# Attention stage of a hybrid encoder step: sums and transposes in halves of one bank, more places for the sums' copy, later output transposes

## The chip, the cores and the metric

The kernel runs on one core of a Trainium2 chip. The metric is the device time of one execution in microseconds (us); less is better. Engine names: TensorE is PE in the profile (its weight loads are PEld), VectorE is DVE, ScalarE is ACT, GpSimd is POOL, SyncE is SP, which issues the DMAs here.

## What is computed

One layer of an encoder step for 1024 prompt frames and 64 sample frames of width 1024. The combined input projection feeds three head groups: six heads of forgetting attention (softmax, called fox), a gated MLP over 128-frame chunks (sgu), and six heads of stick-breaking attention (sb). Their outputs are normalised per head and go through one output projection; then follow a layer norm, a squared-ReLU MLP of width 4096 and a second layer norm. What the change touches is the attention:

```python
def fox_block(q, c_q, qpos, k, v, c_k):
    s = jnp.einsum('bqhd,bkhd->bhqk', q, k) / math.sqrt(D_HEAD)
    s = s + c_q - c_k
    p = jax.nn.softmax(jnp.where(mask, s, NEG_INF), axis=-1)
    return jnp.einsum('bhqk,bkhd->bqhd', p, v)

def sb_block(q, qpos, k, v):
    z = jnp.einsum('bqhd,bkhd->bhqk', q, k) / math.sqrt(D_HEAD)
    log_rem = jnp.where(mask, jax.nn.log_sigmoid(-z), 0.0)
    after = lax.cumsum(log_rem, axis=3, reverse=True) - log_rem
    a = jnp.where(mask, jnp.exp(jax.nn.log_sigmoid(z) + after), 0.0)
    return jnp.einsum('bhqk,bkhd->bqhd', a, v)
```

The arithmetic is float32: a matrix product is made of passes over high and low parts of its operands (`PASSES`).

## The kernel before

The kernel has three stages. The first interleaves all input projections (a generator `fill`) with the attention of both groups (a generator `attn`); a loop at its end asks now one and now the other for its next step by running costs. The second is the output projection with the first norm (`mix`), whose first two row blocks are still asked for by `fill`. The third is the MLP.

A scheduling layer under the kernel orders each engine's instructions by its own estimate of times and by the buffers that are free, and derives the semaphores. So the order in which the kernel's lines are traced is a proposal: the built program may hold another.

Attention runs by pairs of heads (three fox pairs, then three sb pairs); each pair has units (u, h): query block pair u of four, head h of two, and at the end one unit for the sample frames. A unit has three parts:

- `a_steps`: scores of two blocks of 128 queries into banks with tag `s` (L561), then the weights: for fox T by VectorE and an exponential, for sb sg and sn by two sigmoids, a scan (L545) and a product on GpSimd (L547).
- `b_steps`: the weights are transposed 256 keys at a time into banks `pt` (L609) and copied as high and low parts into `pth` by ScalarE (L577) and VectorE (L98). Four products (L619 to L622) add them to the unit's sum `o` of 128 x 256, which takes one bank. Then ScalarE copies the sum into `osb` (L632), which has one place.
- `c_step`: the copy is transposed by two instructions (L640) into `otp`, in the bank with tag `tr`; VectorE adds its high and low halves into `ot` (L641), and after the second head a DMA stores `ot` in DRAM.

The bank `tr` is also used for the transposes of the keys: `pk` (L486) for the prompt and the cached keys (`pkc`, L678) for the sample. `o` is also used by the sample's sum (L741, L745). Each of the tags `o` and `tr` has one bank (bufs=1).

`attn` traces a unit's `b_steps` and the next unit's `a_steps` by turns. A unit's `c_step` goes on a list, which is worked off while the next unit's steps are traced:

```python
                    k += 1
                    if k == 2 and c_pend:
                        while c_pend:
                            c_pend.pop(0)()
```

`prep` loads rows of `o_dr` and of the gates `uu` for the output projection; for the first two row blocks (MIXED) `uu` lies in the pool `sa` with two places.

Of the kernel before, what the change touches and what calls it, by code (L numbers as in the profile page):

```python
# [12 lines left out]
F32 = mybir.dt.float32  # L13
# [7 lines left out]
P = 128  # L21
# [35 lines left out]
def _build(nc, tc, a, es):  # L57
# [117 lines left out]
    def prep(t, sa):  # L175
        n = trows(t)
        o = two_halves(f"oo{t}", sa, "kp")
        if sa is not None:
            uu = sa.tile([P, 256], F32, name=f"uu{t}", tag="uu", bufs=2)
            sqs = [sa.tile([P, 512], F32, name=f"sq{t}", tag="sq", bufs=1)] * 2  # L180
        else:
            uu = sp.tile([P, 256], F32, name=f"uu{t}", tag="gl", bufs=3)
            sqs = [sp.tile([P, 512], F32, name=f"sq{t}_{i}", tag="raw", bufs=2) for i in range(2)]
        nc.sync.dma_start(uu[0:n], u_dr[t * P:t * P + n, :])
        ss = sp.tile([P, 16], F32, name=f"ss{t}", tag="ss", bufs=2)
        for i in range(2):
            oh = o[i][0:n]
            nc.sync.dma_start(oh, o_dr[t * P:t * P + n, i * 512:(i + 1) * 512])
            c = slice(384, 512) if i == 0 else slice(0, 128)
            nc.gpsimd.tensor_tensor(oh[:, c], oh[:, c], uu[0:n, i * P:(i + 1) * P], op=ALU.mult)  # L190
            sq = sqs[i]
            nc.scalar.activation(sq[0:n], oh, AF.Square)
            sh = ss[0:n, i * 8:(i + 1) * 8]
            nc.vector.tensor_reduce(sh, sq[0:n].rearrange("p (h c) -> p h c", c=DH), axis=AX.X, op=ALU.add)
            nc.vector.scalar_tensor_tensor(sh, sh, 1.0 / DH, env["rge"][0:n, t, i * 8:(i + 1) * 8],
                                           op0=ALU.mult, op1=ALU.add)
            nc.gpsimd.tensor_tensor(sh, sh, negh[0:n].broadcast_to([n, 8]), op=ALU.pow)
            o3 = oh.rearrange("p (h c) -> p h c", c=DH)
            nc.vector.tensor_tensor(o3, o3, sh.unsqueeze(2).broadcast_to([n, 8, DH]), op=ALU.mult)
        os_[t] = o  # L200
# [83 lines left out]
    ps = es.enter_context(tc.tile_pool(name="ps", bufs=2, space=PSUM))  # L284
# [4 lines left out]
    gmx = sp.tile([P, KT], F32, name="gmx")  # L289
    with ExitStack() as p1:  # L290
        sa = p1.enter_context(tc.tile_pool(name="sa", bufs=1, side="right"))
        sel2 = sa.tile([TS, P], F32R, name="sel2")
        nc.vector.tensor_copy(sel2[:, 0:TS], ident[0:TS, 0:TS])
        nc.vector.tensor_copy(sel2[:, TS:P], ident[0:TS, 0:TS])
# [156 lines left out]
        def kv_stage(st, tiles, kpiece, vpiece):  # L451
            j, wkv, nv = st["nm"], st["wkv"], st["nv"]
            kcol = st["hp"] * P
            kvs = []
            for i, t in enumerate(tiles):
                n = trows(t)
                if st["first"]:
                    x_trans(t, xrs[t])
                acc = ps.tile([P, 512], F32, name=f"kv{j}_{t}", tag="acc", bufs=2)
                yield from tok_mm(acc, 0, wkv, t, 0, nv)  # L460
                kv = sa.tile([P, 256], F32, name=f"kvs{j}_{t}", tag="kvs", bufs=2)
                kvs.append(kv)
                nc.scalar.activation(kv[0:n], acc[0:n, 0:256], AF.Copy)
                if nv > 256:
                    nc.vector.tensor_copy(fx[0:n, t, :], acc[0:n, 256:262])
                if t == NB:
                    fold(nc.vector, kv[0:n], acc, 0, 256)
                    if nv > 256:
                        fold(nc.vector, fx[0:n, t, :], acc, 256, 6)
                g = 0 if t < NB else 1  # L470
                r0 = t * P if t < NB else 0
                nc.sync.dma_start(flat(st["ok"][g])[r0:r0 + n, kcol:kcol + P], kv[0:n, 0:P])
                nc.sync.dma_start(flat(st["ov"][g])[r0:r0 + n, kcol:kcol + P], kv[0:n, P:2 * P])
                vs = kv[0:n, P:2 * P].rearrange("p (h c) -> p h c", h=2)
                vh = vpiece[0:n, i, :, 0:DH]
                nc.gpsimd.tensor_copy(vh, vs)
                lo_sub(nc.gpsimd, vpiece[0:n, i, :, DH:P], vs, vh)
                if i + 1 < len(tiles):
                    yield 0.109 * 8

            def finish():
                tot = 0
                pk = ps.tile([P, 2 * P], F32, name=f"pk{j}_{tiles[0]}", tag="tr", bufs=1)
                for kv, t in zip(kvs, tiles):
                    n = trows(t)
                    nc.tensor.transpose(pk[:, tot:tot + n], kv[0:n, 0:P], ident[0:n, 0:n])  # L486
                    tot += n
                k_stack(pk[:, 0:tot], kpiece, tot, f"{j}_{tiles[0]}")

            later.append(finish)  # L490
            yield 0.109 * 8

# [87 lines left out]
        class Unit:  # L580
# [18 lines left out]
            def b_steps(self):  # L599
                st, u, h, rows = self.st, self.u, self.h, self.rows  # L600
                nm = f"{st['nm']}_{u}_{h}"
                o = ps.tile([P, 256], F32, name=f"o{nm}", tag="o", bufs=1)
                pths = {}

                def tr(m):
# [22 lines left out]
                    av(m - 1)  # L628
                    yield 0.88
                av(u)  # L630
                osb = sa.tile([P, 256], F32, name=f"osb{nm}", tag="osb", bufs=1)
                nc.scalar.activation(osb, o, AF.Copy)  # L632

                def c_step():
                    if h == 0:
                        st["ot"] = sa.tile([P, 2, P], F32, name=f"ot{nm}", tag="ot", bufs=1)
                    ot = st["ot"]
                    otp = ps.tile([P, 2, P], F32, name=f"otp{nm}", tag="tr", bufs=1)
                    for half in range(2):
                        nc.tensor.transpose(otp[:, half, :], osb[:, half * P:(half + 1) * P], ident)  # L640
                    nc.vector.tensor_reduce(ot[:, :, h * DH:(h + 1) * DH],  # L641
                                            otp.rearrange("p q (s c) -> p q c s", s=2), axis=AX.X, op=ALU.add)
                    if h == 1:
                        oc = st["ocol"]
                        nc.sync.dma_start(o_dr[u * 256:(u + 1) * 256, oc:oc + P].rearrange("(q p) c -> p q c", p=P), ot)
                        written.add((st["nm"], u))
# [6 lines left out]
        class Sample:  # L653
# [16 lines left out]
            def prep_steps(self):  # L670
                st = self.st
                nm = st["nm"]
                self.kc = [sa.tile([P, 2, 256], F32R, name=f"kc_{nm}_{m}", tag="kp", bufs=10) for m in range(2)]
                self.vc = [sa.tile([P, 2, 2, P], F32R, name=f"vc_{nm}_{m}", tag="vp", bufs=10) for m in range(2)]
                for m in range(2):
                    pk = ps.tile([P, 256], F32, name=f"pkc{nm}_{m}", tag="tr", bufs=1)
                    for t in range(2):
                        nc.tensor.transpose(pk[:, t * P:(t + 1) * P], self.kr[m][:, t, :], ident)  # L678
                    k_stack(pk, self.kc[m], 256, f"c{nm}_{m}")
                    for t in range(2):  # L680
                        vh, vl = self.vc[m][:, t, :, 0:DH], self.vc[m][:, t, :, DH:P]
                        vr = self.vr[m][:, t, :].rearrange("p (h c) -> p h c", h=2)
                        nc.gpsimd.tensor_copy(vh, vr)
                        lo_sub(nc.gpsimd, vl, vr, vh)
                    yield 0.22
# [37 lines left out]
            def b_steps(self):  # L723
                st = self.st
                nm, vn, vc, row = st["nm"], st["vn"], self.vc, self.row
                nk = PAST + TS
                o = ps.tile([P, 256], F32, name=f"os{nm}", tag="o", bufs=1)
                pt = ps.tile([P, 512], F32, name=f"pts{nm}", tag="pt", bufs=2)
                for kb in range(NPB):
                    nc.tensor.transpose(pt[:, kb * P:(kb + 1) * P], row[:, kb * P:(kb + 1) * P], ident)  # L730
# [264 lines left out]
        def attn():  # L995
# [39 lines left out]
            def settle(x):  # L1035
# [7 lines left out]
                if x[1] == 4:  # L1043
                    live["kn"] -= 1

            nxt = a_of(seq[0])
            yield from nxt
            for i, x in enumerate(seq):
                b = x[3].b_steps()
                nxt = a_of(seq[i + 1]) if i + 1 < len(seq) else iter(())  # L1050
                alive = [nxt, b]
                k = 0
                while alive:
                    g = alive[k % len(alive)]
                    try:
                        c = next(g)
                    except StopIteration:
                        alive.remove(g)
                        continue
                    if isinstance(c, tuple) and c not in done:  # L1060
                        for cb_ in b:
                            yield cb_
                        settle(x)
                    yield c
                    k += 1
                    if k == 2 and c_pend:
                        while c_pend:
                            c_pend.pop(0)()
                settle(x)
            while c_pend:  # L1070
                c_pend.pop(0)()

        c_pend = []
        nc.scalar.preload_act_table_set("natural_log_exp_and_others")
# [1059 lines left out]
```

## Time and profile before

| | us |
|---|---|
| median of 3 runs | 1394.44 |
| lowest and highest | 1392.70, 1396.25 |
| the profiled execution | 1397.22 |
| its span, first to last instruction | 1395.4 |
| mean granted TensorE clock in it | 0.984 of full speed |

The profile is of one execution. Engine times in it are busy times within the span; a wait is an engine's idle time, told with the instruction that ended it. The granted clock is the share of TensorE's full speed that the throttle allowed. L-numbers are lines of the kernel before; L98 is a helper that subtracts a high part (`lo_sub`).

### The profile page before, as it was taken

The page shows a single profiled execution, that of the slowest core. Times are in us where ns is not written, and L with a number is a line of the kernel's source. Part 1 is how long each engine was busy: PE and PEld are TensorE (multiplying, and loading weights), DVE is VectorE, ACT ScalarE, POOL GpSimd, SP SyncE. Part 2 cuts the span into 40 slices and gives each one's busy share as a digit, 9 for nine tenths or more (in the row PEclk, how much of TensorE's full clock was granted, in tenths as well). Part 3 has the DMA queues.
Part 4 walks back from the last instruction along what each step waited for, and adds up shares of the span by engine and source line. Part 5 has one row for each costly group of instructions (what it writes and reads, how often), then busy time and mean ns, then how long its engine had stood idle before and what let it go on. Part 6 is the DMA issues. An engine that isn't in the chain of part 4 may idle for free.

```text
span 1395.4 us, 24328 instructions
## 1 busy us (share of the span) xinstructions
PE 1327.3 (95%) x8827; PEld 1206.7 (86%) x8827; DVE 1002.8 (72%) x1795; ACT 719.7 (52%) x1561; POOL 609.4 (44%) x667
## 2 busy tenths in 40 slices
PE   7999999999898998999889999999998999999996
PEld 7899989999888988877789999999986788887775
DVE  3577566576788279779966868777678677767677
ACT  4366565566556376334523223223266676767675
POOL 3222231245665445656412212212167675565557
PEclk9999999999999999999999999999999999999999
DMA  7445564231403247532234344343468334334333
GB/s 220 98 128 155 155 207 119 67 78 43 102 12 70 66 145 247 178 106 76 76 114 142 117 168 140 118 167 132 166 217 289 123 138 166 129 128 155 99 136 128
DMA packets 159088, 185.64 MB, mean 133 GB/s; under 512 B 27756, under 2 KB 117164, under 8 KB 158968
## 3 DMA queue, kind: packets, MB, share of 16 engines
q1 hardware_dynamic: 158968, 184.08, 41.8%
q8 instruction: 70, 1.15, 0.4%
q14 instruction: 50, 0.41, 0.1%
HBM read 117.65 MB, written 60.10 MB: 127 GB/s over the span
## 4 chain that ended last, share of the span: by engine, by line
PE 61%; DVE 12%; DMA 9%; ACT 6%; POOL 5%; issue 4%; SPq 1%; ACTq 0%; DVEq 0%; POOLq 0%
PE zA L1294 9%; PE A L1756 7%; PE zD L1294 6%; PE kvsb L362 5%; PE mx L251 4%; PE D L1756 3%; PE zB L1294 3%; PE zC L1294 3%; PE kvfox L362 3%; DMA rwo<-w_out 2%; PE B L1756 2%; POOL wd L98 2%; PE qfox L503 1%; PE qsb L503 1%; DMA xr<-x_prompt 1%
## 5 line engine op out<-in xcount | busy, mean ns | idle before, releaser
L98 POOL TENSOR_TENSOR wa<-wr,wa 128x512 fp32r<-128x512 f32 x42 | 63.9, 1547 | 227.7 <-ACT wa L1232 227.7
L98 POOL TENSOR_TENSOR wd<-rd,wd 128x512 fp32r<-128x512 f32 x77 | 100.4, 1315 | 108.7 <-ACT wd L1232 100.1
L251 PE MATMUL mx<-xT,oTb 128*128 128x512 f32 (+1 forms) x416 | 104.1, 402 | 0.6 <-DVE oTb L98 0.6
L1294 PE MATMUL zA<-xo,ws 128*128 128x288 f32 (+1 forms) x720 | 98.4, 291 | 4.6 <-ACT sn L1305 4.6
L1294 PE MATMUL zD<-xo,ws 128*128 128x288 f32 (+1 forms) x720 | 98.6, 291 | 2.6 <-DVE hh L1308 1.5
L1294 PEld LDWEIGHTS zA<-xo,ws 128*128 128x128 f32 x720 | 94.5, 191 | 4.8 <-ACT sn L1305 4.8
L1294 PEld LDWEIGHTS zD<-xo,ws 128*128 128x128 f32 x720 | 94.5, 190 | 3.3 <-DVE hh L1308 2.0
L362 PE MATMUL kvfox<-wkvfox,xT 128*128 128x256 f32 (+3 forms) x624 | 92.2, 297 | 1.1 <-ACT wkvfox L338 0.5
L1426 POOL TENSOR_TENSOR rd<-rd 128x512 f32<-128x512 f32 x56 | 79.4, 1417 | 30.9 <-DVE b L98 28.6
L251 PEld LDWEIGHTS mx<-xT,oTb 128*128 128x128 f32 (+1 forms) x416 | 75.7, 187 | 18.7 <-DVE oTb L98 1.1
L547 POOL TENSOR_TENSOR sgsb<-sgsb,snsb 128x127 f32<-128x127 f32 (+7 forms) x48 | 58.4, 1218 | 75.8 <-DVE snsb L545 68.6
L362 PE MATMUL kvsb<-wkvsb,xT 128*128 128x256 f32 (+1 forms) x624 | 89.3, 288 | 0.0
L1232 ACT ACTIVATE wd<-rd 128x512 fp32r<-128x512 f32 x105 | 63.6, 623 | 46.9 <-POOL rd L1426 22.7
L1756 PE MATMUL A<-wd,wd 128*128 128x512 f32 x312 | 83.4, 396 | 3.2 <-DVE acc L1723 2.3
L362 PEld LDWEIGHTS kvfox<-wkvfox,xT 128*128 128x128 f32 (+1 forms) x624 | 83.0, 196 | 3.0 <-ACT wkvfox L338 0.9
L545 DVE TENSOR_TENSOR_SCAN snsb<-snsb,one 128x128 f32<-128x128 f32 (+7 forms) x48 | 72.4, 1512 | 14.9 <-ACT snsb L544 14.2
L362 PEld LDWEIGHTS kvsb<-wkvsb,xT 128*128 128x128 f32 (+1 forms) x624 | 80.3, 189 | 0.2
L1305 ACT ACTIVATE sn<-zA 128x256 f32<-128x256 f32 (+1 forms) x80 | 31.0, 390 | 87.8 <-PE zA L1294 74.6
L1756 PEld LDWEIGHTS A<-wd,wd 128*128 128x128 f32 x312 | 58.0, 188 | 19.5 <-DVE acc L1723 3.9
L1756 PE MATMUL A<-wd,h4a 128*128 128x512 f32 x240 | 65.1, 395 | 1.4 <-DVE acc L1723 0.6
L1514 ACT ACTIVATE ws<-wr 128x1024 fp32r<-128x1024 f32 x28 | 29.2, 1058 | 59.2 <-DVE wr L1244 59.2
L1756 PEld LDWEIGHTS A<-wd,h4a 128*128 128x128 f32 x240 | 44.5, 188 | 13.9 <-ACT wd L1232 1.0
(548 smaller groups left out, 3752.9 us busy)
## 6 DMA issues: line engine op xcount, KB each, us to landing
h_dr<-hh SPq DMA_DIRECT2D x30, 512.0 KB, 3.2
rd<-w_down SPq DMA_DIRECT2D x30, 512.0 KB, 4.4
wr<-w_up SPq DMA_DIRECT2D x13, 1024.0 KB, 5.5
hr<-h_dr SPq DMA_DIRECT2D x31, 384.0 KB, 4.4
h_dr<-hh SPq DMA_DIRECT2D x30, 384.0 KB, 3.6
raw<-w_in SPq DMA_DIRECT2D x44, 256.0 KB, 3.5
wo_dr<-swo SPq DMA_DIRECT2D x32, 256.0 KB, 2.5
xT<-wo_dr SPq DMA_DIRECT2D x8, 1024.0 KB, 7.9
```

Of the source, the lines that this page charges most:

```text
L98: eng.tensor_tensor(out, src, hi.bitcast(F32), op=ALU.subtract)
L251: nc.tensor.matmul(acc[0:m], oT[:, k, hx, 0:m], wo[k // 4][hw][:, k % 4, cs], start=(i == 0), stop=(i == len(seq) - 1))
L362: nc.tensor.matmul(acc[0:n, c0:c0 + n1 - n0], xT[k // 4][:, k % 4, c:c + n], wt[:, k, hw, n0:n1], start=(i == 0), stop=(i == len(seq) - 1))
L503: nc.tensor.matmul(acc[:, 0:w], wq[:, k, hw, :], xT[k // 4][:, k % 4, c:c + w], start=(i == 0), stop=(i == len(seq) - 1))
L545: nc.vector.tensor_tensor_scan(g[:, 0:n][:, ::-1], g[:, 0:n][:, ::-1], one.broadcast_to([P, n]), 1.0, op0=ALU.mult, op1=ALU.bypass)
L547: nc.gpsimd.tensor_tensor(s[:, 0:n - 1], s[:, 0:n - 1], g[:, 1:n], op=ALU.mult)
L1232: nc.scalar.activation(hi, raw, AF.Copy)
L1294: nc.tensor.matmul(z, w[:, hw, k], xop(s, bo, hx)[:, k, :], start=(new and k == 0 and j == 0), stop=(k == 3 and j == 2), skip_group_check= ...
L1305: nc.scalar.activation(c, z, AF.Copy)
L1426: eng.tensor_tensor(r[:, o], r[:, x], r[:, y], op=ALU.subtract)
L1514: nc.scalar.activation(ws[:, 0, q, c], src[:, q], AF.Copy)
L1756: nc.tensor.matmul(z, h[:, hx, q, o], wset[self.c % 2][q][:, hw, wb], start=((n in (0, 3) or n == 1 and self.c == 0) and q == 0 and j == 0 ...
```

## The change

It does four things:

- The tags `o` and `tr` each get one tile of a whole bank (128 x 512), made once, and `half_bank` gives out its left and right 256 columns by turns: for the sums `o` of the units and of the samples, for the keys' transposes `pk` and `pkc`, and for the outputs' transposes `otp`.
- The sums' copy `osb` moves to the tag `uu`, which now has three places, shared with the `uu` tiles of `prep`.
- The `c_step` of a unit is traced after three steps of the next instead of two.
- What is still on the list when a unit's steps have ended is worked off there.

```diff
-            uu = sa.tile([P, 256], F32, name=f"uu{t}", tag="uu", bufs=2)
+            uu = sa.tile([P, 256], F32, name=f"uu{t}", tag="uu", bufs=3)
...
+        halves = {}
+
+        def half_bank(tag):
+            if tag not in halves:
+                halves[tag] = [ps.tile([P, 512], F32, name=f"{tag}2", tag=tag, bufs=1), 0]
+            b, k = halves[tag]
+            halves[tag][1] = 1 - k
+            return b[:, k * 256:(k + 1) * 256]
...
-                pk = ps.tile([P, 2 * P], F32, name=f"pk{j}_{tiles[0]}", tag="tr", bufs=1)
+                pk = half_bank("tr")
...
-                o = ps.tile([P, 256], F32, name=f"o{nm}", tag="o", bufs=1)
+                o = half_bank("o")
...
-                osb = sa.tile([P, 256], F32, name=f"osb{nm}", tag="osb", bufs=1)
+                osb = sa.tile([P, 256], F32, name=f"osb{nm}", tag="uu", bufs=3)
...
-                    otp = ps.tile([P, 2, P], F32, name=f"otp{nm}", tag="tr", bufs=1)
+                    otp = half_bank("tr").rearrange("p (a b) -> p a b", a=2)
...
-                    pk = ps.tile([P, 256], F32, name=f"pkc{nm}_{m}", tag="tr", bufs=1)
+                    pk = half_bank("tr")
...
-                o = ps.tile([P, 256], F32, name=f"os{nm}", tag="o", bufs=1)
+                o = half_bank("o")
...
+            def turn():
+                while c_pend:
+                    c_pend.pop(0)()
...
-                    if k == 2 and c_pend:
-                        while c_pend:
-                            c_pend.pop(0)()
+                    if k == 3:
+                        turn()
+                turn()
                 settle(x)
-            while c_pend:
-                c_pend.pop(0)()
+            turn()
```

## The prediction

> **What bounds the kernel now.** I read the first part of the page, then the chain of waits, then the stretches of 100 us, then what TensorE itself waited for up to 600 us, then short stretches around single waits.
>
> ```profile
> span 1395.4 us, 24328 instructions
> PE 1327.3 (95%) x8827; PEld 1206.7 (86%) x8827; DVE 1002.8 (72%) x1795; ACT 719.7 (52%) x1561; POOL 609.4 (44%) x667
> PE 61%; DVE 12%; DMA 9%; ACT 6%; POOL 5%; issue 4%; SPq 1%; ACTq 0%; DVEq 0%; POOLq 0%
> ```
>
> TensorE is the bound: 95% busy, and the largest part of the chain that ended last. The changed edits all lie in the first stage, input projections interleaved with attention, which ends near 570 us. There the question is how long TensorE stood still.
>
> ```profile
> core 0: us, PE busy (x) PEld busy (x) DVE busy (x) ACT busy (x) POOL busy (x), PEclk, DMA share, GB/s
> 200.00:300.00 100.00, 97.96 (x789) 94.10 (x788) 64.33 (x169) 60.44 (x152) 30.39 (x50) 1.00 0.37 99
> 300.00:400.00 100.00, 93.15 (x747) 91.02 (x746) 72.14 (x124) 61.34 (x158) 60.53 (x82) 0.97 0.25 64
> 400.00:500.00 100.00, 91.22 (x703) 87.24 (x703) 66.75 (x115) 52.96 (x137) 53.75 (x74) 0.95 0.27 68
> 500.00:560.00 60.00, 54.25 (x403) 51.27 (x401) 49.70 (x77) 39.18 (x98) 30.26 (x27) 0.92 0.63 211
> 560.00:600.00 40.00, 40.00 (x196) 32.81 (x195) 31.32 (x57) 14.19 (x27) 28.81 (x31) 1.00 0.46 144
> ```
>
> Columns: stretch, its length, each engine's busy time and count, then granted clock. From 200 to 300 us TensorE issues 789 instructions, one each 0.127 us (100 / 789); this is my unit below. From 300 to 560 us it stands still for 6.9 + 8.8 + 5.8 = 21.5 us (lengths less busy times), and the granted clock falls to 0.92 to 0.97. In the last row it no longer waits. All that this change can win or lose lies in those idle times and the clock drops.
>
> ```profile
> PE osb L621 <- DVE pthsb L98: 5.3, 9, 1.7
> PE otpsb L640 <- ACT osbsb L632: 5.0, 4, 1.7
> ...
> PE sgv L362 <- DVE sgvv L761: 1.9, 1, 1.9
> PE osb L619 <- ACT pthsb L577: 1.8, 2, 1.6
> PE osb L619 <- ACT osbsb L632: 1.7, 1, 1.7
> PE Sfox L561 <- DVE mfox L533: 1.4, 3, 0.7
> PE Ssb L561 <- ACT snsb L544: 1.4, 2, 1.1
> ...
> PE pkcsb L678 <- DVE otsb L641: 0.8, 1, 0.8
> PE sgm L808 <- ACT so L812: 0.8, 2, 0.6
> PE pksb L486 <- DVE kc_sb L98: 0.6, 1, 0.6
> ...
> PE ofox L619 <- ACT osbfox L632: 0.5, 1, 0.5
> ...
> PE otpfox L640 <- ACT osbfox L632: 0.2, 1, 0.2
> ```
>
> Each line: who waited <- for whom, us in total, times, longest. The change aims at the lines with osb (the sums' copy) and at the two that wait for the bank of transposes: 5.0 + 1.7 + 0.5 + 0.2 = 7.4 us for the copy and 0.8 + 0.6 = 1.4 us for the bank, 8.8 us together.
>
> A wait costs more than itself:
>
> ```profile
> 304.10:307.50 3.40, 3.40 (x19) 3.40 (x18) 2.23 (x5) 2.76 (x10) 2.69 (x6) 0.51 0.45 116
> 307.50:310.90 3.40, 3.40 (x31) 3.40 (x30) 1.61 (x3) 1.35 (x4) 2.04 (x3) 0.99 0.00 0
> ...
> 382.60:386.00 3.40, 3.40 (x17) 3.24 (x17) 2.72 (x9) 1.69 (x6) 2.25 (x8) 0.51 0.34 82
> ...
> 553.30:560.10 6.80, 6.09 (x24) 5.33 (x25) 6.43 (x15) 3.43 (x8) 5.17 (x4) 0.50 0.98 339
> 560.10:566.90 6.80, 6.80 (x37) 5.63 (x36) 3.94 (x7) 2.82 (x7) 3.90 (x5) 1.00 0.68 231
> ```
>
> ```profile
> 303.62 0.39 PE L619 MATMUL osb<-pthsb,vpsb 128*128 128x256 f32 x1 [1.73 <-ACT osbsb L632]
> ```
>
> Right behind the 1.7 us wait for osbsb at 303.6 us the clock is granted at 0.51 for 3.4 us, and TensorE does 19 instructions where the next 3.4 us hold 31. The 12 missing ones at 3.40 / 31 = 0.110 us are 1.3 us. The same comes at 382 us. The double stretch at 553 us loses 37 - 24 = 13 at 6.80 / 37 = 0.184, 2.4 us, its own 0.7 us of idle included.
>
> **The change, part by part.** The built program holds the same instructions as before on every engine; what differs is their order (on TensorE from the 730th of its 8827 instructions to the 4247th, about 105 to 580 us) and the waits. So nothing is added or removed in work: the sum consists of waits alone.
>
> *Two halves for the sums (o).* Meant: the next sum is accumulated in one half while ScalarE still copies the other. But both halves are one tile in one bank, and the built program keeps order on the bank: following the waits, I find that in all 48 units the first product into a half still stands behind the copy of the sum before it, in the other half. Gain: 0.
>
> The rows cannot show two halves at work, since in the kernel before each sum has the bank alone; their bound is the 1.7 + 0.5 us above. [...]
>
> *Two halves for the transposes (tr).* The same: the next transposes into the other half still stand behind the readers of the half before. Gain 0 of the 1.4 us.
>
> *Three places for the copy, shared with uu.* Before, a copy had to wait until the copy before it had been transposed. How often did that hold a copy back?
>
> ```profile
> L632 ACT ACTIVATE osbfox<-ofox x24: 360/380/420, 76.9 to 285.2; 128x256 f32<-128x256 f32 x24
> ...
>   PE ofox L622: 7.0, 4
>   PE otpfox L640: 1.3, 1
> ```
> ```profile
> 202.09 0.39 ACT L632 ACTIVATE osbfox<-ofox 128x256 f32<-128x256 f32 x1 [1.34 <-PE otpfox L640]
> ```
> ```profile
> L184 SPq DMA_DIRECT2D uu<-u_dr x9: 319/332/535, 530.5 to 591.3; - x9
> ```
>
> ScalarE stood idle once, 1.3 us at 202 us, for the transposes (otpfox); its other waits were for the sum itself. All that TensorE waited for osbfox is the 0.7 us above, wherever it fell. So the single place is no limit: gain 0, at most 0.7. The first loads into uu come at 530.5 us, when three sums remain, and in the built program no copy waits for a uu's reader, so sharing costs 0 too.
>
> *Transposes one step later, and the order that follows.* What decides whether TensorE waits for a copy is how many instructions lie between a sum's last product and the first that needs its copy. Before, the four otpsb waits of 1.25 us stand at distances of 5, 8, 8 and 14: 8.75 x 0.127 = 1.1 us, so a copy is there about 2.4 us (some 19 instructions) after the sum. Counting, in the built programs, what each distance below 20 lacks: stick-breaking units lack 78 before (distances 5, 8, 8, 8, 8, 11, 14) and 87 after (5, 6, 10, 11, 12, 12, 12, 13, 16, 18, 18). Scaled by what 78 cost (5.0 + 1.7 = 6.7 us), that is 6.7 x 87 / 78 = 7.5, or +0.8 us. Softmax units lack 34 before (8, 11, 12, 15) and 67 after (4, 7, 8, 9, 12, 17, 17, 19). Before, that cost 0.7, so +0.7 us; at the full 0.127 each it would be 33 x 0.127 = +4.2. I take the scaled value, because ScalarE reaches these copies sooner, as the small 0.7 shows. So this edit, which should give the copy more time, gives less: the scheduler has pulled later work forward to where it thought buffers to be free.
>
> Other moves, by the same counting. The stick-breaking products that waited 1.1 us at 502 us (row below) now have twelve gate matmuls (sgu) ahead of them: -1.1 us. The gate products (sgm, 0.8 us) lack 48 to a distance of 16 where they lacked 27: 0.8 x 48 / 27 = 1.4, +0.6 us. The second output projection now starts 5 instead of 24 instructions behind its transposes; the nearest row is
>
> ```profile
> L251 PE MATMUL mx<-xT,oTb 128*128 128x512 f32 (+1 forms) x416 | 104.1, 402 | 0.6 <-DVE oTb L98 0.6
> ```
>
> so +0.6 us, with 0 and 1.2 as bounds. The waits for pthsb (5.3 + 1.8 us) lack 131 to 16 before and after: 0. The sgv wait keeps its distance: 0.
>
> ```profile
> 501.85 1.02 PE L561 MATMUL Ssb<-kpsb,qdsb 128*128 128x256 f32 x4 [1.08 <-ACT snsb L544]
> ```
>
> *Clock.* One wait of over 1 us goes (502 us), one comes (the sample's sum after the fourth pair of the second softmax heads, at a distance of 4): 0, with 1.3 us either way.
>
> Sum: 0.8 + 0.7 - 1.1 + 0.6 + 0.6 = +1.6 us. The profiled execution took 1397.2 us (its span 1395.4), 2.8 above the median 1394.4; 1397.2 + 1.6 = 1398.8 in its own terms, 1396.0 as a median.
>
> **The rivals.**
>
> *The halves work.* If the bank did not bind, all 8.8 us of waits go, with the clock drops at 304 and 382 us (2 x 1.3): -11.4, 1383.0; with two double drops of 2.4 more, 1378.2. Against it: the built waits on the bank. Chance 0.04.
>
> *The new order falls well.* The total lack is like before, but which instruction is late also depends on ScalarE's and VectorE's queues, which are reordered in some 270 and 330 places. If the copies are reached as soon as in the softmax units (0.7 us for a lack of 34, against 6.7 for 78), the osbsb waits shrink to 87 / 34 x 0.7 = 1.8 us: -4.9, and two clock drops of 1.3 go: -7.5, 1386.9. For: some distances grew (8 to 16 at 304 us). Against: most did not. Chance 0.16.
>
> *Slower: waits spread, and each drops the clock.* Before, the softmax heads ran at full clock from 200 to 300 us. After, their shortest distances are 4, 7 and 9, and a stick-breaking sum at 423 us has gone from 33 to 12. If four such places each wait 1.25 us (the osbsb mean) and each halves the clock for 3.4 us (1.3 us), that is 4 x 2.55 = +10.2, 1404.6. It decides from the point where a wait reaches about 1.1 us: in the trace such waits have drops behind them, the 0.5 us ones don't. For: the distances. Against: copies there came early. Chance 0.32.
>
> That the change does nothing it says (no overlap) is the forecast itself: only order remains. Chance 0.48.
>
> **How the numbers follow.** Forecast 1396.0. The range, 1387 to 1405, reaches to the second and third rival; left out are the halves at work (0.04) and the outer parts of those two (about 0.15). A measurement here tells 0.3%, 4.2 us, from no change. Faster by more: 0.04 + 0.16 = 0.20; within: 0.48; slower: 0.32. The forecast case alone spans 1391 to 1399.
>
> **What would show it right or wrong.** In the waits of TensorE, first products and transposes behind osb copies should still total 6 to 10 us in about ten places; were they under 2 us, the halves work and the first rival holds. The counts of the groups should not change. Between 200 and 300 us the granted clock at 1.00 speaks for the forecast, under 0.97 for the third rival. The wait of Ssb for snsb near 502 us should be gone, and a wait of an os product for osbfox near 206 us should have come. After 600 us nothing should differ; if it does, my statement that only the first stage is touched is wrong.

## The result: 0.64% slower, and the profile after

The changed kernel took 1402.21 us in the median of 7 runs (1398.87 to 1409.31), the kernel before 1394.44 us beside it. The ratio is 1.0064, with an interval of 1.0047 to 1.0081. That is 8 to 9 us slower: inside the range, but on the side of the third rival and not where the likeliest case lay. Its profiled execution took 1401.5 us. Lines of the changed kernel stand ten further down than those of the kernel before (L621 is now L631, L640 is L650), and the sum and transposes are called `o` and `tr`.

The head of the page after, its first part and its chain:

```profile
span 1399.8 us, 24356 instructions
PE 1326.6 (95%) x8827; PEld 1209.1 (86%) x8827; DVE 1000.7 (71%) x1795; ACT 720.7 (51%) x1561; POOL 615.7 (44%) x667
PE 62%; DVE 12%; DMA 10%; ACT 5%; issue 5%; POOL 4%; SPq 1%; ACTq 0%; DVEq 0%; POOLq 0%
```

The counts of the engines are the same, and TensorE's busy time nearly so (1327.3 us before). What grew lies outside its work. The stretches of 100 us, with the same columns as before:

```profile
200.00:300.00 100.00, 96.36 (x758) 93.19 (x757) 61.20 (x165) 57.66 (x144) 25.85 (x46) 0.97 0.37 102
300.00:400.00 100.00, 92.78 (x735) 89.17 (x734) 71.62 (x121) 61.65 (x158) 60.24 (x81) 0.97 0.25 64
400.00:500.00 100.00, 91.03 (x697) 87.10 (x696) 63.86 (x109) 50.16 (x130) 56.63 (x73) 0.95 0.21 53
500.00:560.00 60.00, 54.46 (x445) 52.39 (x445) 53.28 (x85) 43.33 (x108) 32.24 (x30) 1.00 0.62 211
560.00:600.00 40.00, 36.68 (x169) 29.26 (x170) 29.34 (x56) 14.13 (x28) 28.58 (x27) 0.91 0.55 174
```

Between 200 and 300 us TensorE got through 758 instructions instead of 789, at a clock of 0.97 instead of 1.00. And the last row, which had no idle time before, now has 3.3 us of it. What TensorE waited for up to 600 us, in the changed kernel:

```profile
PE o L631 <- DVE pthsb L98: 9.8, 9, 2.2
...
PE Sfox L571 <- DVE mfox L543: 3.4, 4, 2.3
...
PE mx L251 <- DVE oTb L98: 1.4, 1, 1.4
PE tr L650 <- ACT osbfox L642: 1.2, 1, 1.2
PE mx L251 <- ACT oTb L209: 1.2, 2, 0.7
PE o L629 <- ACT osbsb L642: 1.1, 1, 1.1
PE o L751 <- ACT osbfox L642: 1.0, 1, 1.0
...
PE tr L650 <- ACT osbsb L642: 0.6, 1, 0.6
PE sgm L818 <- ACT so L822: 0.5, 1, 0.5
```

The waits for the sums' copy fell from 7.4 to 3.9 us (1.2 + 1.1 + 1.0 + 0.6), below the 6 to 10 us that the prediction named. So the copies did get more time. Others took their place: pthsb in this line 5.3 to 9.8, mfox 1.4 to 3.4, and the second output projection (mx for oTb), which had no such wait up to 600 us, 2.6 (1.4 + 1.2).

### The profile page after: what moved, and what is told of

It reads as the page before. It is cut to its first block, busy times and chain, and to the rows that moved or that the text cites. A ratio compares the mean times of both kernels' runs of the same rounds, so it can differ in the third digit from the quotient of the medians.

```text
span 1399.8 us, 24356 instructions
## 1 busy us (share of the span) xinstructions
PE 1326.6 (95%) x8827; PEld 1209.1 (86%) x8827; DVE 1000.7 (71%) x1795; ACT 720.7 (51%) x1561; POOL 615.7 (44%) x667
## 4 chain that ended last, share of the span: by engine, by line
PE 62%; DVE 12%; DMA 10%; ACT 5%; issue 5%; POOL 4%; SPq 1%; ACTq 0%; DVEq 0%; POOLq 0%
PE A L1769 10%; PE zA L1307 9%; PE zD L1307 6%; PE D L1769 5%; PE kvsb L372 5%; PE zB L1307 3%; PE zC L1307 3%; PE mx L251 3%; DMA rwo<-w_out 3%; PE kvfox L372 2%; PE B L1769 2%; DVE snsb L555 2%; PE qfox L513 1%; DMA raw<-w_in 1%; PE ds L1815 1%
## 5 line engine op out<-in xcount | busy, mean ns | idle before, releaser
L1439 POOL TENSOR_TENSOR rd<-rd 128x512 f32<-128x512 f32 x56 | 79.6, 1421 | 29.6 <-DVE b L98 27.3
L1736 DVE TENSOR_TENSOR acc<-acc,A 128x512 f32<-128x512 f32 x73 | 49.0, 679 | 8.9 <-PE A L1769 8.9
```

The costliest lines, as they stand in the source:

```text
L1439: eng.tensor_tensor(r[:, o], r[:, x], r[:, y], op=ALU.subtract)
L1736: nc.vector.tensor_tensor(out, out if other is None else other, bank, op=ALU.add)
```

## The experiments

Theory A: only the order of instructions costs, and it costs through TensorE's idle time and the half-clock stretches behind it. Its rivals: a shared bank, shared places, or one engine's backlog costs by itself.

Twelve runs, each timed over five rounds. For each I also read one stretch of the trace, from TensorE's 730th to its 4271st instruction (about 107 to 600 us): the same 3541 instructions in every kernel but for one or two at its ends, in one order or another. "Idle" is TensorE's idle time in it, "half" the time at half clock, both summed from the trace's records.

| kernel | order | ratio to before, interval | stretch us | idle | half |
|---|---|---|---|---|---|
| before | old | | 490.9 | 26.5 | 27.3 |
| halves_only | old | 0.9985 [0.9969, 1.0001] | 488.1 | 27.8 | 17.1 |
| all_edits_old_order | old | 0.9994 [0.9981, 1.0006] | 485.4 | 26.0 | 17.1 |
| old_order_moves | old, 14 moves | 0.9997 [0.9981, 1.0014] | 488.2 | 27.3 | 17.1 |
| old_order_gate_on_pool | old | 1.0013 [1.0000, 1.0026] | 493.1 | 28.4 | 27.3 |
| new_then_old | new to 350 us | 1.0014 [1.0004, 1.0024] | 490.7 | 29.9 | 23.9 |
| places_only | its own | 1.0047 [1.0026, 1.0067] | 496.2 | 30.4 | 30.7 |
| later_only | its own | 1.0051 [1.0030, 1.0071] | 495.9 | 34.3 | 20.5 |
| after | new | 1.0064 [1.0047, 1.0081] | 499.4 | 32.9 | 34.1 |
| places_and_later | new | 1.0069 [1.0048, 1.0090] | 496.9 | 33.7 | 23.9 |
| new_order_low_first | new, 5 moves | 1.0084 [1.0064, 1.0104] | 498.1 | 33.2 | 30.7 |
| new_order_all_moves | new, 11 moves | 1.0078 [1.0058, 1.0098] | 497.5 | 33.0 | 27.3 |
| new_order_gate_on_pool | new | 1.0047 [1.0031, 1.0064] | 493.0 | 33.5 | 13.7 |
| earlier_only | its own | 1.0119 [1.0099, 1.0139] | 505.7 | 38.8 | 34.1 |

The rows can be added up. A half-clock window of 3.4 us costs 1.3 us (the prediction's count of missing instructions), which is 0.39 of it. Stretch less idle less 0.39 x half is 451.5 to 454.3 us in all fourteen rows. A fit to the rows with both factors left free gives nearly the same: 1.03 for idle time and 0.37 for half clock. So the loss is idle time and clock, to within 1.5 us. Of old order (before, halves_only, all_edits_old_order) against new (after, places_and_later), in means: stretch 488.1 to 498.2, +10.0; idle 26.8 to 33.3, +6.5; half 20.5 to 29.0, +8.5 x 0.39 = +3.3. Within one order, "half" alone varies from 17 to 27 or 24 to 34 us, which is 4 us of time; it may be much of the scatter between executions.

### Each edit by itself

Only the half banks (`half_bank("o")` and `half_bank("tr")` in place of the tiles; nothing else):

> Only the half banks of the sums and of the transposes; copies keep their one place and the transposes their step. Theory A (the 7.8 us come from the new order of instructions, and the halves are inert): the built program has the order of the kernel before on every engine, so 1394 us, ratio 1.000 within 0.002, and the waits for osb's copy stay near 7.4 us. Rival B (the shared bank itself costs, as two engines in one bank): slower by 4 to 8 us, ratio 1.003 to 1.006, though nothing is reordered. Rival C (the halves do overlap a copy with the next sum): 11 us faster, ratio 0.992.

Its order is that of the kernel before on every engine, its time too. The waits for copies:

```profile
PE tr L650 <- ACT osbsb L642: 5.0, 4, 1.7
...
PE o L629 <- ACT osbsb L642: 1.5, 1, 1.5
...
PE o L629 <- ACT osbfox L642: 0.4, 1, 0.4
```

6.9 us where it was 7.2 without the smallest line. Working halves could shorten only the waits of the first products, since the transposes need the copy itself: these are 1.9 us (1.5 + 0.4) where they were 2.2, so next to nothing overlaps. Rivals B and C fall. The waits, unchanged to 0.3 us, agree with what the prediction found in the built program: in all 48 units the next sum stands behind the copy of the one before. What the halves would do without that order, no run shows.

The other two edits without the halves:

> The other two edits, without the half banks: copies in three places shared with uu, and the transposes one step later. Theory A: its order is that of the changed kernel on every engine, so ratio 1.0064 within 0.002 (1402 us), with waits of L621's products (first stage) for VectorE's pthsb near 9.8 us and a clock below 1.00 between 200 and 300 us, as in the changed kernel. Rival B: the halves were the cost, so 1.000 to 1.003. Rival C: the halves won something that hid a larger loss, so slower than the changed kernel, above 1.009.

1.0069: as the changed kernel, with nearly the same waits (pthsb 10.2 us, mfox 3.4, copies 3.4). The halves have no part in the loss.

```diff
-                osb = sa.tile([P, 256], F32, name=f"osb{nm}", tag="osb", bufs=1)
+                osb = sa.tile([P, 256], F32, name=f"osb{nm}", tag="uu", bufs=3)
```

> Only the three places for the sums' copy, shared with uu; the transposes keep their step. TensorE's order differs from before in 601 instructions, from the 1426th on. Theory A (order decides, each edit adds waits of its own): no later than the changed kernel, and the part up to TensorE's 1426th instruction (about 200 us) as before; ratio between 1.000 and 1.004. Rival (the sharing itself holds a copy back until a uu is read): ACT waits at the copies and a ratio near 1.0064 by this edit alone.

```diff
-                    if k == 2 and c_pend:
+                    if k == 3:
```

> Only the transposes one step later, with the one place for the copy kept. TensorE's order differs in 1200 instructions, from the 729th on. Theory A: the larger part of the 7.8 us, ratio 1.003 to 1.007, through new waits of 1 to 2 us (for pthsb, mfox, copies) with half-clock stretches behind them. Rival D (the later step alone is harmless and only together with the places does the order fall badly): 1.000 within 0.002. Rival E (with one place the next copy must now wait longer for the later transposes): ACT waits before the copies grow from 1.3 us to 5 us or more, and PE waits for the copies with them, ratio above 1.007.

Either edit alone costs three quarters of the whole (1.0047, 1.0051), so the parts do not add up: each gives the scheduler another start, and each gets an order of its own. places_only was expected at 1.004 at most and came out above it, with 1.004 still inside its interval. Both rivals about the buffers fall: in places_only no copy waits for the reader of a uu, and in later_only the copies wait for a transpose 1.3 us in all, as before.

### The buffers without the order

All edits' buffers, with the transposes traced at the old step; after tracing, `keep_order` adds a dependency from each instruction of the first stage to the one ahead of it in the old order, on every engine:

```diff
         build(tc, aps)
+        keep_order(nc, tc)
```

> All the buffers of the changed kernel (half banks, three places for the copy shared with uu), but every engine is held to the instruction order of the kernel before by explicit dependencies from one instruction to the next. Theory A (only the order costs): 1394 us, ratio 1.000 within 0.002, TensorE's waits as in the kernel before: 7.4 us for copies, 7 us for pthsb, 1.4 us for mfox. Rival (sharing the places with uu, or the one tile per bank, costs by itself): as slow as the changed kernel, 1.004 to 1.007.

0.9994. This settles the first question: with half banks and shared places and the old order the loss is gone. That `keep_order` does not gain by itself shows in the runs below, which hold the new order with it and stay slow. The reverse, the old buffers with the new order, was not tried.

### Taking single waits away

What made the largest new waits? TensorE at 420 us in the changed kernel, and VectorE in the same time (start, duration, instruction):

```profile
420.71 0.33 PE L631 MATMUL o<-pthsb,vpsb 128*128 128x128 f32 x1 [2.04 <-DVE pthsb L98]
```
```profile
417.91 1.63 DVE L846 TENSOR_SCALAR sgvv<-sgvv,sgst 128x256 f32<-128x256 f32 x1
419.45 0.41 DVE L842 BATCH_NORM_STATS2 sgst<-sgvv 128x6 f32<-128x256 f32 x1
419.79 0.40 DVE L847 TENSOR_TENSOR sgvv<-sgvv,gvb 128x256 f32<-128x256 f32 x1
420.11 0.55 DVE L98 TENSOR_TENSOR pthsb<-ptsb,pthsb 128x384 fp32r<-128x384 f32 x1
```

VectorE does not idle here: gate operations stand ahead of the low part for which TensorE waits. The first of them, L846, also lasted 1.63 us, where it took 0.40 us at 445 us. GpSimd ran a product beside it:

```profile
417.84 1.54 POOL L557 TENSOR_TENSOR sgsb<-sgsb,snsb 128x767 f32<-128x767 f32 x1
```

It ended at 419.38 us and L846 at 419.54. In the traces of the kernels before and after, nine of these gate instructions lasted 0.73 to 1.63 us where the others of their size took 0.38 to 0.45, and each of the nine ended 0.15 us behind a GpSimd instruction. In the stretch, all VectorE instructions that lasted over 0.2 us longer than quick ones of their kind overlapped a GpSimd instruction; they lost 21.1 us together before and 23.3 after. So VectorE's queue also gets longer where GpSimd works beside it: L846 took 1.63 us there, and 0.40 us at 445 us, where no GpSimd instruction ran with it. How much of a wait this is, no run here singles out.

Near 229 us it is an instruction that itself waits for a DMA, with the copy behind it on ScalarE and TensorE's transposes behind the copy:

```profile
228.86 0.72 ACT L991 ACTIVATE swo<-rwo,gmx 128x512 fp32r<-128x512 f32 x1 [1.44 <-DMA rwo<-w_out]
229.48 0.36 ACT L642 ACTIVATE osbfox<-o 128x256 f32<-128x256 f32 x1
229.90 0.44 PE L650 MATMUL tr<-ident,osbfox 128*128 128x128 f32 x2 [1.19 <-ACT osbfox L642]
```

The largest wait for mfox came the same way. VectorE's part of such a scaling of output weights (swo) waited for ScalarE's, and the mask and the row maximum (mfox) stood behind it:

```profile
187.04 0.75 DVE L992 SCALAR_TENSOR_TENSOR swo<-rwo,gmx,swo 128x512 fp32r<-128x512 f32 x1 [1.73 <-ACT swo L991]
188.94 1.20 PE L571 MATMUL Sfox<-kpfox,qdfox 128*128 128x256 f32 x4 [2.27 <-DVE mfox L543]
```

So I moved what TensorE waits for ahead of such instructions. The first of five moves in the list of the order, put in words (the list itself holds numbers of instructions):

```diff
-  scan snsb, mask Ssb, reduce otsb, pthsb low part
+  pthsb low part, scan snsb, mask Ssb, reduce otsb
```

> The changed kernel with its own order on every engine, but for five moves on VectorE: the low part of pthsb (L98), on which a waiting product of TensorE hangs near 386, 420, 450, 540 and 560 us, goes ahead of what stands before it in VectorE's queue (a scan of 1.46 us and two short ones; four gate operations of 2.7 us together; two of 1.3 us; 0.4 us; two of 0.8 us). Theory A (the waits for pthsb are made by what was put ahead of them): TensorE's wait for pthsb in L631 falls from 9.8 us by 4 to 6.5 us, and with it two to four half-clock stretches of 1.3 us: 5 to 11 us faster than the changed kernel, 1391 to 1397 us, ratio to the kernel before 0.998 to 1.002. Rival (the delayed scan or gate step only makes another wait as long): within 2 us of the changed kernel, ratio 1.005 to 1.008.

> As the run before, and six further moves in the changed kernel's order: ScalarE's copies osb (near 187, 206, 229 and 555 us) and the mask and row maximum of fox scores on VectorE (near 188 and 230 us) go ahead of an instruction that waits for a DMA (scaling of output weights swo, L991 and L992, of wkvsb, L348) or of one exponent step. In the trace these waiting instructions held the engine for 1.4 to 2.3 us while TensorE waited 2.27, 1.03, 1.19, 0.66 and 1.07 us. Theory A: a further 3 to 6 us of TensorE's idle time and up to three half-clock stretches go: 1384 to 1394 us, ratio 0.993 to 1.000. Rival (the delayed instructions make waits of their own): no faster than the run before.

> The kernel before, its own order held on every engine, but for fourteen moves of one or two places on ScalarE and VectorE: what TensorE waits for (six copies or low parts held behind a qss copy, a gate step or a weight split that itself waits, and others) goes ahead of that. The waits at these places in the kernel before add up to 15.6 us; by what stood ahead of each, up to 12 us of it can go, and of its six half-clock places up to five. Theory A (TensorE's idle time in the first stage is made by what was queued ahead on the engines that it waits for, whatever the number of places for copies): 6 to 18 us faster, 1376 to 1388 us, ratio 0.987 to 0.996. Rival (the waits are set by the sum's last product and the copy's own duration, so order on the other engines changes little): ratio 0.998 to 1.001.

The moves did what they should, and none of the three gained anything (1.0084, 1.0078, 0.9997; expected were 0.998 to 1.002, 0.993 to 1.000, 0.987 to 0.996). The waits of new_order_low_first:

```profile
PE o L631 <- DVE pthsb L98: 3.4, 7, 1.2
PE wstp L804 <- POOL wsr L792: 2.7, 2, 1.9
...
PE sgm L818 <- ACT so L822: 2.0, 2, 1.5
...
PE sgu L372 <- DVE up L872: 1.7, 1, 1.7
```

The wait for pthsb fell by 6.4 us, and in the stretch TensorE's idle time rose from 32.9 to 33.2. At 384 us the wait of 2.2 is down to 0.32, and four instructions later TensorE waits 1.86 us for GpSimd's wsr. At 418 us 2.04 are gone, and here is what follows:

```profile
416.84 0.50 PE L818 MATMUL sgm<-vh,wst 128*128 128x256 f32 x2 [0.55 <-DVE sgvv L771]
420.36 0.50 PE L818 MATMUL sgm<-vh,wst 128*128 128x256 f32 x2 [1.54 <-ACT so L822]
421.50 0.44 PE L650 MATMUL tr<-ident,osbsb 128*128 128x128 f32 x2 [0.53 <-ACT osbsb L642]
```

TensorE came to the next result earlier, and that was not ready earlier. Near 537 us the displaced g1u (L769) took 2.06 us where it had taken 0.40 (it ended 0.28 us behind a product on GpSimd), and sgu, with no such line before, waits 1.7 us for the up behind it. old_order_moves shows the same: its waits for osbsb fell from 6.7 to 2.9 us, while those for Tfox grew from 1.1 to 2.4 and those of the transposes for otsb (1.8) and of sgm for vh (1.0) came anew. In new_order_all_moves the wait for mfox fell from 3.4 to 0.7 us, and one of 3.1 us for the high part pthfox came. So the rivals of the first two hold. That of old_order_moves had the right time for another reason: it expected the waits to stay, and they moved. Here a wait that ended last hid the ones behind it.

### A hybrid of the two orders

The same trick with the new order up to TensorE's 2621st instruction and the old one after it:

> Places and later step, every engine held to the changed kernel's order up to TensorE's 2621st instruction (about 350 us) and to the kernel before's order after that. Theory A' (the time of a stretch is a constant plus TensorE's idle time plus 0.39 of its half-clock time, and each order costs where it stands): up to there as the changed kernel, +1 to +4 us against before; from there as before, so without the 4.3 us that the new order cost between the 2621st and the 3348th instruction and the 3.2 us at the second output projection: in all 1.001 to 1.003, 1395.5 to 1398 us. Rival (waits taken out at one place come back at the next, as the moved low parts showed): as slow as the changed kernel, 1.005 to 1.008.

1.0014, as expected: from there on the stretches are those of the kernel before. Two of them bounded by the same instructions, the 2622nd to the 3349th and the 4136th to the 4271st, in the kernel before, the changed one and this one:

```profile
349.94:457.01 107.07, 95.69 (x728) 91.41 (x727) 85.67 (x155) 63.03 (x164) 65.12 (x81) 0.94 0.28 67
...
570.43:597.91 27.48, 27.48 (x137) 22.55 (x135) 23.27 (x45) 9.72 (x17) 22.03 (x24) 1.00 0.44 131
```
```profile
352.61:463.46 110.85, 97.21 (x728) 91.84 (x727) 86.64 (x154) 63.52 (x163) 67.28 (x80) 0.94 0.26 64
...
576.34:606.21 29.87, 28.00 (x136) 22.37 (x135) 23.63 (x45) 9.98 (x17) 24.85 (x25) 1.00 0.41 118
```
```profile
352.65:460.46 107.81, 95.72 (x728) 91.42 (x727) 85.91 (x154) 62.99 (x163) 65.42 (x81) 0.94 0.27 67
...
573.91:601.39 27.48, 27.48 (x136) 22.54 (x135) 23.37 (x45) 9.83 (x17) 22.19 (x24) 1.00 0.43 132
```

The first took 107.07, 110.85 and 107.81 us, the second 27.48, 29.87 and 27.48. So these parts of the cost sit where the new order stands: 3.8 us among the second stick-breaking heads, 2.4 in the output projection. From the 730th to the 2622nd instruction, in the new order, the hybrid's execution took 242.0 us, the one before 242.9 and the changed one 245.8. It had 2.4 us more idle time there than before (10.3 to 7.9) but no half-clock window, so what the early part costs this one execution doesn't settle. Exchanging a whole stretch of order on all engines does what exchanging one instruction on one engine did not.

### Less work for VectorE

In the first of these stretches VectorE is busy for 80% (85.67 of 107.07). If its backlog set the waits, less work would end them:

```diff
-                nc.vector.tensor_tensor(v[0:n], v[0:n], gv[0:n], op=ALU.mult)
+                nc.gpsimd.tensor_tensor(v[0:n], v[0:n], gv[0:n], op=ALU.mult)
```

> The changed kernel in its own order, but the gate's multiplication by g_v (nine operations, 0.88 us each on VectorE between 390 and 460 us) runs on GpSimd, directly ahead of the addition there. Theory V (between 350 and 457 us TensorE waits for VectorE's backlog, 80% busy there, whichever operation is the late one): VectorE loses 8 us of work in that stretch, TensorE's idle time there falls from 13 us by 3 to 6 us and a half-clock window or two with it: 1.000 to 1.004. Rival O (only order counts, or GpSimd becomes the late one, at 0.77 us for each of the nine): within 0.002 of the changed kernel, 1.0045 to 1.0085.

> The same move of nine multiplications to GpSimd in the kernel before, its order held. Theory V: TensorE's 11.2 us of idle time between its 2621st and 3348th instruction falls by 3 to 5 us: 0.995 to 0.998, faster than both kernels. Rival O: 0.999 to 1.002; if GpSimd becomes the late one, above 1.002.

The same stretch, in the new order and then in the old:

```profile
350.32:458.70 108.38, 95.69 (x729) 89.34 (x728) 80.00 (x145) 63.19 (x163) 72.94 (x89) 0.97 0.27 66
```
```profile
350.39:459.80 109.41, 97.34 (x729) 92.61 (x728) 79.93 (x146) 63.49 (x164) 71.75 (x90) 0.92 0.27 66
```

VectorE lost 6.6 and 5.7 us. TensorE's idle time in the stretch went from 13.6 to 12.7 us and from 11.4 to 12.1: no 3 us in either. In the new order fewer windows fell to half clock (13.7 to 6.8 us), and 1.0047 is lower than the 1.0064 of the same order, but the intervals overlap. Theory V falls: it isn't VectorE's amount of work alone. GpSimd had 5.7 and 6.6 us more to do in the stretch, so the work was shifted here, not taken away.

### The step the other way

```diff
-                    if k == 2 and c_pend:
+                    if k == 1 and c_pend:
```

> The kernel before with the output transposes traced one step earlier (after one step of the next unit instead of two), nothing held: a third order by the scheduler. Theory A'' (an order that the scheduler lays out anew costs a few us whichever way the step goes, since it does not know these waits): 1.002 to 1.008. Rival (the cost comes from going later, so going earlier gains): 0.995 to 1.000.

1.0119, the slowest of all, beyond the range given. So it isn't "later" alone that costs. Its waits are again others:

```profile
PE ofox L619 <- ACT pthfox L577: 5.0, 3, 2.4
...
PE mx L251 <- DVE oTb L98: 3.7, 2, 2.5
...
PE Ss0sb L699 <- DVE kc_sb L98: 2.4, 2, 1.9
```

Four orders that the scheduler laid out anew (places, later, both, earlier) cost 0.5 to 1.2%. Why each of them is worse than the old one, I can't say from these runs. No version was faster than both kernels by more than its interval.

## Why the prediction was right or wrong

The time lies in the range because the range was drawn out to the third rival, and not by the sum: of its five terms only one came out near its forecast, and two that were set to 0, pthsb and the clock, grew.

**Halves, and the built waits on the bank: right.** Gain 0 was forecast for both tags; halves_only has the old order, the old waits and the old time.

**Places and sharing: right as a resource, wrong as an edit.** all_edits_old_order confirms that the places cost and gain nothing. But the prediction put all of the new order on the later transposes; the places alone reorder 601 TensorE instructions and cost 0.47%.

**Copy waits, +0.8 and +0.7: failed for the stick-breaking heads.** They fell from 6.7 to 1.7 us; for the softmax heads they rose from 0.7 to 2.2, the sample's sum near 207 us (1.0) among them, as named. The step counted TensorE's instructions between a sum and its first use, and scaled by what one case had cost. Between them lies ScalarE's queue: at 229 us a copy stood behind an instruction that waited 1.44 us for a DMA, and TensorE waited 1.19 us for the copy. The distance on TensorE doesn't say that.

**Waits for pthsb, 0: failed.** The two lines of the forecast rose from 7.1 to 10.8 us (5.3 + 1.8 to 9.8 + 1.0), by 3.7 us at the same distances, through VectorE's queue (420 us). The same holds for mfox, +2.0, which the sum didn't have at all. But the moves showed that these lines are not prices either: with 6.4 us of them taken away, nothing was gained. A sum of single waits, each costed alone, was the deeper error.

**Second output projection, +0.6 with 1.2 as upper bound: mis-sized.** The 0.6 us of the nearest row stand at 650 us; up to 600 us there was no such wait before and 2.6 us after. The group's row after, for the whole span, idle time ahead of it last:

```profile
L251 PE MATMUL mx<-xT,oTb 128*128 128x512 f32 (+1 forms) x416 | 105.8, 405 | 3.3 <-DVE oTb L98 2.1
```

**Ssb at 502 us, -1.1: right** for that wait; with two short ones elsewhere the line fell by 0.7. **The gate products, +0.6: failed, small:** 0.8 to 0.7 (0.5 + 0.2). **sgv, 0: right** (1.9 to 2.1).

**Clock, 0 with 1.3 either way: failed.** +2.7 us in the stretch for the two profiled executions (half 27.3 to 34.1), +3.3 in the means. The price of a window, 1.3 us (0.39 x 3.4), agrees with the free fit (0.37).

**The third rival** came nearest: waits in the softmax heads, each with a half clock behind it (189, 209 and 233 us): 10.2 us at half clock in all, which by 0.39 cost 4.0 us. Its place was only partly right. The hybrid shows that of the stretches read, the larger part lay among the stick-breaking heads and in the projection. Its point of decision, 1.1 us, was wrong, and the trace before already spoke against it: the waits of 1.55 us at 361 us and 1.14 us at 493 us had no half clock behind them. The last section has what decides. And its sign, the clock from 200 to 300 us, is a poor one: places_and_later, with the same order and the same loss, had 1.00 there.

**After 600 us nothing should differ: nearly.** The order is the same. The 604 us mark (TensorE's 4261st instruction) is 8.3 us late and the 7001st 8.8; then the last stage of this one execution gives back 4.4. In halves_only and places_and_later the same stage is 2 to 3 us shorter than before, in the same order, so I read it as scatter.

## What to carry to other kernels

More buffers or a later step gave the copies time, and the time was lost elsewhere, because each edit made the scheduler lay out the stage anew: compare an edit with the order held fixed before crediting or blaming it. The wait that a profile names can be only the last to end (at 384 us one of 2.2 us fell to 0.32, and 1.86 us for another input followed); before pricing its removal, look for the next instruction on that engine that has an input from elsewhere, since moving such instructions ahead at eleven and at fourteen places gained nothing. Time could be split into a constant, idle time and half-clock time to within 1.5 us, and so one profiled execution of each kernel showed where an order has its idle time; the clock's part still varied by 4 us between executions.

## What the runs showed of the clock

The half-clock stretches are not a matter of one wait's length. In the traces of the kernels before and after, the clock's records up to 640 us hold 0.50 or 1.00 of full speed and nothing between, and each record at 0.50 lasts 3.413 or 6.827 us. In every trace their starts lie on a grid of 3.413 us, to within a hundredth of a window. Cut by this grid from 60 to 640 us, over fourteen traces: of 65 full-clock windows in which TensorE was busy for less than half, 60 were followed by a half-clock one; of 91 with 0.5 to 0.7 busy, 19; of 2122 above 0.7, none. (In those two traces alone: 10 of 10, 4 of 12, 0 of 296.) The same wait for mfox before the same score product shows it. In the changed kernel it lies in one window:

```profile
182.00:185.40 3.40, 3.40 (x32) 3.40 (x31) 2.72 (x7) 1.81 (x4) 0.00 (x0) 1.00 0.74 222
185.40:188.80 3.40, 1.26 (x12) 1.06 (x10) 1.69 (x5) 1.59 (x3) 0.00 (x0) 1.00 0.46 152
188.80:192.20 3.40, 3.27 (x15) 3.29 (x16) 3.03 (x8) 1.62 (x3) 0.00 (x0) 0.50 0.79 220
```

In later_only it is 2.05 us long and falls across two windows:

```profile
185.40:188.80 3.40, 2.40 (x21) 2.20 (x20) 1.35 (x5) 1.91 (x5) 0.00 (x0) 1.00 0.47 137
188.80:192.20 3.40, 2.35 (x18) 2.23 (x19) 3.37 (x10) 1.89 (x4) 0.00 (x0) 1.00 0.88 261
192.20:195.60 3.40, 2.29 (x17) 1.95 (x17) 1.93 (x5) 2.19 (x4) 0.00 (x0) 1.00 0.51 162
```

1.26 us busy, and the next window has 15 instructions at 0.50; 2.40 and 2.35 us busy, and the clock stays. So in these traces over 1.7 us of idle time within one window nearly always brought the next one to half clock (60 of 65), 1.0 to 1.7 us in about one case of five (19 of 91), and less never did (0 of 2122). Where the grid lies against the start of the kernel changes from run to run: its first line stands 0.36 us behind the first instruction in the kernel before, 1.09 us in the changed one.
